# A diffusion step with two scans per head: the first levels of the scans set between the products of the paired projections

## The chip, the cores and the metric

The kernel runs on one core of a Trainium2 chip. Its engines are TensorE (PE in the profile; PEld is its loading of weights), VectorE (DVE), ScalarE (ACT), GpSimd (POOL) and SyncE (SP), which issues nearly all DMAs from one queue, in order. The metric is device time in microseconds of one execution.

## The reference, cut to what matters

One layer on 1152 tokens (128 context, 1024 latent) of width 1024. One input projection feeds eight heads of a gated scan in both directions and a Fourier branch with four groups; both are gated, projected, merged and projected once more.

```python
proj = h @ w_in
q, ff, fb, vi, zA, u, zB, gA, gB = jnp.split(proj, SPLITS, axis=-1)
qh = jax.nn.silu(heads(q)); vh = heads(vi)
logf_f, k_f = forget_gate(heads(ff), lb_f)      # k = 1 - f
logf_b, k_b = forget_gate(heads(fb), lb_b)
# per head and direction, token by token: S = diag(f) S + k v^T, o = S^T q
o = o_f + o_b_rev[:, ::-1]
o = o * lax.rsqrt(jnp.mean(o * o, axis=-1, keepdims=True) + EPS) * gnorm_w
yA = o.reshape(B, L, D_A) * jax.nn.silu(zA)
yF = jnp.fft.fft2(ug, axes=(1, 3), norm='ortho').real
yB = yF * jax.nn.silu(zB)
merged = jax.nn.sigmoid(gA) * (yA @ w_pa) + jax.nn.sigmoid(gB) * (yB @ w_pb)
return merged @ w_o, S_f, S_b
```

## The kernel before

**The stages.** A startup normalises the input and splits every value into a high and a low part, so that three products of reduced precision give one of full precision (`mm3`, lines 197 to 199: high by high, low by high, high by low). Then come the **paired projections**: 27 calls of `pair`, two output blocks of 128 columns each. A pair computes seven block products instead of eight, each for two halves j of 576 columns in slices of 288, so it has 14 products of 12 matmuls. Its weights are loaded into one buffer `raw` (512 KB twice) and turned into seven blocks: a11, a12, a22 straight from `raw`, and four sums s1 to s4 (lines 538, 540, 542, 546, VectorE). Each block is split (line 525 on ScalarE for the high part, line 526 on GpSimd for the low part). VectorE joins the seven products with seven additions for each half (line 551). An activation follows, and the result goes to DRAM. The forget gates take a Sigmoid on ScalarE and a multiply and add on GpSimd (lines 592, 593). The Fourier branch is a generator, `four`, of which the pairs run one step after each half.

**The scan stage.** Then come the eight heads. A head has six levels within blocks of 32 tokens (0, 1, 2, 4, 8, 16; `scan_blocks`): each takes 36 matmuls of 32x32 into `s_ps` (line 188), a merge into `a32` (lines 698, 700), and for the levels from 1 on two copies that pick halves (`km`, `qm`, lines 686, 688, ScalarE) and three multiplications that carry the factors on (`grow`: `qq` and `kk` at full length, line 665, and the factors `ff`, line 667, VectorE). Then `scan_rest` does the levels 32 and 64, transposes, the states S, the outputs and the normalisation.

**What sets the order.** Python generators are advanced by a string of letters for each step n (`PATTERN`): E is one level of head n, L a step of `scan_rest` of head n-1, Y a step of the end of head n-2, F one slice of the dense projections of the branches (12 matmuls of 288 columns), V half a slice of the late value projection (12 of 256 columns). The matmuls of the scan stage keep this order; a scheduler places all else by its own estimate of time, and on each engine the instructions then run in that fixed order. Before, a step n from 2 to 7 has six E, nine L, three Y and seven to nine F; there are 20 V, all in the steps 0 and 1.

## Time and profile before

| | us |
|---|---|
| median of 3 runs (1364.75 to 1376.12) | 1366.0 |
| the profiled execution | 1369.38 |
| its span in the trace | 1367.6 |
| mean granted clock of TensorE | 0.954 of 2.4 GHz |

The trace has its times from the start of the span. The startup ends at about 160 us, the paired projections at 806.6, the scan stage at about 1195, and the rest is the last branch products and the output projection.

### The profile page before, as it was taken

The page shows a single profiled execution, that of the slowest core. Times are in us where ns is not written, and L with a number is a line of the kernel's source. Part 1 is how long each engine was busy: PE and PEld are TensorE (multiplying, and loading weights), DVE is VectorE, ACT ScalarE, POOL GpSimd, SP SyncE. Part 2 cuts the span into 40 slices and gives each one's busy share as a digit, 9 for nine tenths or more (in the row PEclk, how much of TensorE's full clock was granted, in tenths as well). Part 3 has the DMA queues.
Part 4 walks back from the last instruction along what each step waited for, and adds up shares of the span by engine and source line. Part 5 has one row for each costly group of instructions (what it writes and reads, how often), then busy time and mean ns, then how long its engine had stood idle before and what let it go on. Part 6 is the DMA issues. An engine that isn't in the chain of part 4 may idle for free. (4 is left out here: it accounts for less than half of the span.)

```text
span 1367.6 us, 31165 instructions
## 1 busy us (share of the span) xinstructions
PE 1257.8 (92%) x12768; PEld 1189.8 (87%) x12768; DVE 853.0 (62%) x1403; ACT 569.4 (42%) x1056; POOL 658.7 (48%) x499
## 2 busy tenths in 40 slices
PE   5999899999999999999999996878787787999998
PEld 2679899999999999999999996877786786999886
DVE  7737744444344344444443478999999999675554
ACT  4542223333333233323332446666666664432332
POOL 4426546555647456558643503321312734464654
PEclk8899999999999999999999998898988898999999
DMA  8542242332443443233423243553445433577332
GB/s 321 195 170 73 69 140 84 119 135 91 130 133 117 154 153 114 84 114 109 157 93 113 85 157 107 179 156 113 138 147 172 119 117 100 153 219 234 119 129 99
DMA packets 102993, 185.04 MB, mean 135 GB/s; under 512 B 9777, under 2 KB 70978, under 8 KB 99650
## 3 DMA queue, kind: packets, MB, share of 16 engines
q1 hardware_dynamic: 102562, 182.00, 40.6%
q8 instruction: 100, 1.64, 0.5%
q10 hardware_dynamic: 288, 1.05, 0.3%
q14 instruction: 43, 0.35, 0.1%
HBM read 132.41 MB, written 50.60 MB: 134 GB/s over the span
## 5 line engine op out<-in xcount | busy, mean ns | idle before, releaser
L174 POOL TENSOR_TENSOR w_lo<-w_raw,w_hi 128x512 fp32r<-128x512 f32 (+1 forms) x36 | 78.7, 2188 | 194.3 <-ACT w_hi L172 164.1
L842 POOL TENSOR_TENSOR merged<-merged,gs 128x288 f32<-128x288 f32 x64 | 72.2, 1138 | 65.6 <-DVE gs L841 65.5
L188 PE MATMUL d_ps<-yh,w_hi 128*128 128x288 f32 x256 | 86.7, 339 | 10.7 <-DVE merged L839 4.9
L665 DVE TENSOR_TENSOR qq<-qq,ff 128x1152 f32<-128x1152 f32 x56 | 91.9, 1653 | 6.9 <-ACT qm L688 6.7
L542 DVE TENSOR_TENSOR sb<-raw 128x512 f32<-128x512 f32 x27 | 21.5, 798 | 112.6 <-DMA raw<-in_w_pr 112.6
L665 DVE TENSOR_TENSOR kk<-kk,ff 128x1152 f32<-128x1152 f32 x56 | 89.9, 1605 | 0.3
L188 PE MATMUL d_ps<-yh,w_lo 128*128 128x288 f32 x256 | 80.6, 315 | 0.5 <-POOL w_lo L174 0.5
L188 PE MATMUL d_ps<-yl,w_hi 128*128 128x288 f32 x256 | 80.5, 314 | 0.0
L593 POOL TENSOR_SCALAR c<-c,omlb,lb 128x576 f32<-128x576 f32 x32 | 28.1, 879 | 107.3 <-ACT c L592 60.5
L526 POOL TENSOR_TENSOR a11l<-raw,a11h 128x512 fp32r<-128x512 f32 x27 | 34.9, 1294 | 74.8 <-ACT a11h L525 74.7
L188 PEld LDWEIGHTS d_ps<-yh,w_hi 128*128 128x128 f32 x256 | 52.9, 207 | 13.5 <-ACT w_hi L172 3.9
L551 DVE TENSOR_TENSOR c<-o_ps,u 128x288 f32<-128x288 f32 x108 | 48.9, 453 | 23.4 <-PE o_ps L199 22.0
L584 ACT ACTIVATE sg<-c 128x576 f32<-128x576 f32 x40 | 27.4, 685 | 84.8 <-DVE c L551 82.4
L551 DVE TENSOR_TENSOR u<-o_ps,m 128x288 f32<-128x288 f32 x36 | 16.3, 454 | 74.3 <-PE o_ps L199 70.3
L686 ACT COPY km<-kk 128x1152 f32<-128x1152 f32 x40 | 51.9, 1297 | 14.3 <-DVE kk L665 7.5
L688 ACT COPY qm<-qq 128x1152 f32<-128x1152 f32 x40 | 52.1, 1302 | 10.1 <-PE s_ps L188 7.1
L188 PE MATMUL o_ps<-S,qq 128*128 128x128 f32 x256 | 44.2, 295 | 12.5 <-DVE S L767 12.5
L188 PEld LDWEIGHTS d_ps<-yh,w_lo 128*128 128x128 f32 x256 | 53.0, 207 | 0.9 <-POOL w_lo L174 0.9
L188 PEld LDWEIGHTS d_ps<-yl,w_hi 128*128 128x128 f32 x256 | 53.4, 209 | 0.0
L526 POOL TENSOR_TENSOR s2l<-sa,s2h 128x512 fp32r<-128x512 f32 x27 | 34.9, 1294 | 32.5 <-ACT s2h L525 32.5
L667 DVE TENSOR_TENSOR ff<-ff 128x1152 f32<-128x1152 f32 (+6 forms) x56 | 50.2, 907 | 0.1
L188 PEld LDWEIGHTS s_ps<-qm,km 128*32 128x32 f32 x2880 | 33.0, 123 | 20.0 <-ACT qm L688 14.0
(405 smaller groups left out, 5044.6 us busy)
## 6 DMA issues: line engine op xcount, KB each, us to landing
raw<-in_w_pr SPq DMA_DIRECT2D x52, 512.0 KB, 4.8
gs<-g_dr SPq DMA_DIRECT2D x96, 144.0 KB, 3.1
w_raw<-in_w_pab SPq DMA_DIRECT2D x44, 256.0 KB, 3.2
f_dr<-c SPq DMA_DIRECT2D x32, 288.0 KB, 2.3
ff<-f_dr SPq DMA_DIRECT2D x8, 1152.0 KB, 6.4
wa<-in_w_ada SPq DMA_DIRECT2D x8, 1024.0 KB
g_dr<-c SPq DMA_DIRECT2D x28, 288.0 KB, 2.9
xs<-in_xT SPq DMA_DIRECT2D x6, 768.0 KB, 9.5
```

The costliest lines, as they stand in the source:

```text
L174: eng.tensor_tensor(out=lo, in0=raw, in1=hi.bitcast(F32), op=ALU.subtract)
L188: queued(nc.tensor.matmul(*args, **kw))
L526: nc.gpsimd.tensor_tensor(out=lo, in0=src, in1=hi.bitcast(F32), op=ALU.subtract)
L542: nc.vector.tensor_tensor(out=sb, in0=a11, in1=a21, op=ALU.subtract)
L551: nc.vector.tensor_tensor(out=out, in0=m, in1=x, op=ALU.add)
L584: nc.scalar.activation(sg, c, AF.Sigmoid)
L593: nc.gpsimd.tensor_scalar(out=c, in0=c, scalar1=omlb[:, i:i + 1], scalar2=lb[:, i:i + 1], op0=ALU.mult, op1=ALU.add)
L665: nc.vector.tensor_tensor(out=xv, in0=xv, in1=view(ff2, off, [[2 * m, T // (2 * m)], [step, 2], [0, m]]), op=ALU.mult)
L667: nc.vector.tensor_tensor(out=fv[0], in0=fv[0], in1=fv[1], op=ALU.mult)
L686: nc.scalar.copy(km.rearrange("p (b i m) -> p b i m", i=2, m=m), view(kk2, 0, dims))
L688: nc.scalar.copy(qm.rearrange("p (b i m) -> p b i m", i=2, m=m), view(qq2, 0, dims))
L842: nc.gpsimd.tensor_tensor(out=out, in0=out, in1=gs, op=ALU.add)
```

## The change

The levels 0, 1, 2 and 4 of all heads leave the scan stage and become a second generator, `pieces`, that is run after `fourier` by the same calls inside the pairs. A head's tokens are cut into two pieces of 640 and 512. A piece loads its factors and q from DRAM, makes `kk`, `qq` and `k0`, does the four levels (with 20 or 16 matmuls each), and stores `kk`, `qq`, the merged blocks and every eighth factor (`fa`) to DRAM. A pair now calls the generator three times in each half (after the products 5, 7 and 2) from the eighth pair on, twice in the pairs 3 to 7. So a piece takes five calls, the 16 pieces 80, at six a pair.

The scan stage loads `kk`, `qq` and `fa` (2.6 MB a head instead of 1.7 MB) into one of three sets of buffers, one head ahead, and does only the levels 8 and 16; `grow` reads the short factors. `PATTERN` has two E in a step, and eight F in each of the steps 2 to 7; the V are ten and ten.

In the pairs, the low parts of the four sums s1 to s4 are made by VectorE, not GpSimd; the third sum is written over `raw`; the second step of the forget gates is done by ScalarE. The pairs that need the Fourier result (zB) are now the last two, behind the gates, and the buffers that hold that result are those into which head 0 is loaded.

```diff
-PATTERN = ['VVVVEEVVVEVVVEVVEVVEVV', 'LEVLEVLLEVVLLEFEFLLLEF', 'LFEFYYYFLEFLLEFLLEFEFLLLEFF', 'LEYYYFLEFLLEFLLEFEFLLLEFF', 'LEFYYYFLFELLEFLLEFEFLLLEFF', 'LEFYYYFLEFLLEFLLEFEFLLLEFF', 'LEFYYYFLFELLEFLLEFEFLLLEFF', 'ELFYYYFLEFLLEFLLEFEFLLELFF', 'LYYFYFLFLLFLLFLLLFFF', 'YFYYFFF']
+EARLY = (1, 2, 4)
+LATE = (8, 16)
+GRAN = 8
+PIECES = ((0, 640), (640, T))
+PATTERN = ['VVVVVVVVEVVE', 'LVVELVVLEVVLVVLVVLFLFLFLF'] + 6 * ['LFEYLFYLFYELFLFLFLFLFL'] + ['LFYLFYLFYLFLFLFLFLFLF', 'YFYFYFF']
 HW = T // 2
+W0 = 1280
+FA = 2 * T // GRAN
...
+    def load_head(p, hd, tags=("kk", "qq", "fa")):
+        kk, qq = (p.tile([P, 2, T], F32, tag=t, name=t) for t in tags[:2])
+        nc.sync.dma_start(kk, kk_dr[hd])
+        nc.sync.dma_start(qq, qq_dr[hd])
+        fa = p.tile([P, FA + NCH * 32], F32, tag=tags[2], name="fa")
+        nc.sync.dma_start(fa, fa_dr[hd])
+        return kk, qq, fa[:, :FA], fa[:, FA:].rearrange("p (c t) -> p c t", t=32)
...
+    def grow(ff, kk, qq, m, w=T, g=1):
+        n, mg, wg = w // (2 * m), m // g, w // g
+        dims = [[2 * m, n], [w + m, 2], [1, m]]
+        for x, off, step in ((qq, wg + mg, -(wg + mg)), (kk, mg, wg - mg)):
+            xv = view(x, 0, dims)
+            nc.vector.tensor_tensor(out=xv, in0=xv, in1=view(ff, off, [[2 * mg, n], [step, 2], [0, m]]), op=ALU.mult)
+        fv = [view(ff, o, [[wg, 2], [2 * mg, n]]) for o in (0, mg)]
+        nc.vector.tensor_tensor(out=fv[0], in0=fv[0], in1=fv[1], op=ALU.mult)
+    def halves(x, km, m, w=T):
+        nc.scalar.copy(km.rearrange("p (b i m) -> p b i m", i=2, m=m), view(x, 0, [[2 * m, w // (2 * m)], [w + m, 2], [1, m]]))
+    def merge(a32, m, ps, n):
+        pv = ps[:, :n * 32].rearrange("p (c t) -> p c t", t=32)
+        if m == 0:
+            nc.vector.tensor_tensor(out=a32, in0=pv, in1=m_d.unsqueeze(1).broadcast_to([P, n, 32]), op=ALU.mult)
+        else:
+            nc.vector.copy_predicated(out=a32, mask=m_i[:, LEVELS.index(m), :].unsqueeze(1).broadcast_to([P, n, 32]), data=pv)
+    def within(ps, km, qm, n, mm):
+        for c in range(n):
+            for j in range(4):
+                ts = slice(c * P + 32 * j, c * P + 32 * j + 32)
+                mm(ps[32 * j:32 * j + 32, c * 32:c * 32 + 32], lhsT=km[:, ts], rhs=qm[:, ts], start=True, stop=True)
...
+    def pieces():
+        x = lp.tile([P, 2, W0], F32, tag="qq", name="px")
+        z = lp.tile([P, 2, W0], F32, tag="kk", name="pz")
+        sm_ = lp.tile([P, 2, 257], F32, tag="tab", name="ps").rearrange("p a b -> p (a b)")
+        todo = [(hd, t0, t1) for hd in range(NH) for t0, t1 in PIECES]
+        def load(hd, t0, t1):
+            w = t1 - t0
+            nc.sync.dma_start(x[:, 0, :2 * w].rearrange("p (d t) -> p d t", d=2), f_dr[hd, :, :, t0:t1])
+            nc.sync.dma_start(z[:, 1, :w], q_dr[hd, :, t0:t1])
+        load(*todo[0])
+        for i, (hd, t0, t1) in enumerate(todo):
+            w, n = t1 - t0, (t1 - t0) // P
+            ff, qq, kk, q, k0 = x[:, 0, :2 * w], x[:, 1, :2 * w], z[:, 0, :2 * w], z[:, 1, :w], z[:, 1, w:2 * w]
+            a32 = sm_[:, :n * 32].rearrange("p (c t) -> p c t", t=32)
+            fa = sm_[:, n * 32:n * 32 + 2 * w // GRAN].rearrange("p (d t) -> p d t", d=2)
+            for d in range(2):
+                ds, es = slice(d * w, (d + 1) * w), slice((1 - d) * w, (2 - d) * w)
+                nc.scalar.activation(kk[:, ds], ff[:, ds], AF.Identity, bias=ones[:, 0:1], scale=-1.0)
+                nc.vector.tensor_tensor(out=qq[:, es], in0=q, in1=ff[:, ds], op=ALU.mult)
+            nc.vector.tensor_tensor(out=k0, in0=kk[:, :w], in1=kk[:, w:], op=ALU.add)
+            yield
+            for m in (0,) + EARLY:
+                if m:
+                    halves(kk, k0, m, w)
+                    halves(qq, q, m, w)
+                    grow(ff, kk, qq, m, w)
+                ps = scan_ps()
+                within(ps, k0, q, n, nc.tensor.matmul)
+                merge(a32, m, ps, n)
+                if m == EARLY[-1]:
+                    nc.scalar.copy(fa, ff.rearrange("p (d t) -> p d t", d=2)[:, :, 0:w:GRAN])
+                    nc.sync.dma_start(kk_dr[hd, :, :, t0:t1], kk.rearrange("p (d t) -> p d t", d=2))
+                    nc.sync.dma_start(qq_dr[hd, :, :, t0:t1], qq.rearrange("p (d t) -> p d t", d=2))
+                    nc.sync.dma_start(fa_dr[hd, :, :FA].rearrange("p (d t) -> p d t", d=2)[:, :, t0 // GRAN:t1 // GRAN], fa)
+                    nc.sync.dma_start(fa_dr[hd, :, FA + t0 // P * 32:FA + t1 // P * 32], sm_[:, :n * 32])
+                    if i + 1 < len(todo):
+                        load(*todo[i + 1])
+                yield
+    four = chain(fourier(), pieces())
...
-            nc.gpsimd.tensor_tensor(out=lo, in0=src, in1=hi.bitcast(F32), op=ALU.subtract)
+            eng = nc.vector if tag[0] == "s" else nc.gpsimd
+            eng.tensor_tensor(out=lo, in0=src, in1=hi.bitcast(F32), op=ALU.subtract)
...
-            sb = sp.tile([P, 4, P], F32, name="sb")
             w = {1: split(a11, "a11")}
             nc.vector.tensor_tensor(out=sa, in0=a21, in1=a22, op=ALU.add)
             w[5] = split(sa, "s1")
             nc.vector.tensor_tensor(out=sa, in0=sa, in1=a11, op=ALU.subtract)
             w[6] = split(sa, "s2")
-            nc.vector.tensor_tensor(out=sb, in0=a11, in1=a21, op=ALU.subtract)
-            w[7] = split(sb, "s3")
+            nc.vector.tensor_tensor(out=a21, in0=a11, in1=a21, op=ALU.subtract)
+            w[7] = split(a21, "s3")
...
+                    if i in (() if n < 3 else (5, 4) if n < 8 else (5, 7, 2)):
+                        next(four, None)
...
-                if n > 2:
-                    next(four, None)
...
-                nc.gpsimd.tensor_scalar(out=c, in0=c, scalar1=omlb[:, i:i + 1], scalar2=lb[:, i:i + 1], op0=ALU.mult,
-                                        op1=ALU.add)
+                nc.scalar.activation(c, c, AF.Identity, bias=lb[:, i:i + 1], scale=omlb[:, i:i + 1])
...
+        for j in range(1, KT):
+            pair(n, ((sigmoid, g_dr[0, j]), (sigmoid, g_dr[1, j])))
+            n += 1
+        for _ in four:
+            pass
+        yfs = [lp.tile([P, 2, T], F32, tag=t, name="yfs") for t in ("kk", "qq")]
...
-        first = load_head(lp, 0)
+        first = load_head(lp, 0, ("kk", "qq", "tab"))
...
-    def scan_blocks(hd, ff, q):
...
+    def scan_blocks(hd, kk, qq, fa, a32):
+        kk2, qq2 = flat(kk), flat(qq)
+        for m in LATE:
+            km = s0[0].tile([P, T], F32, name="km", bufs=2)
+            halves(kk2, km, m)
+            qm = s0[0].tile([P, T], F32, name="qm", bufs=1)
+            halves(qq2, qm, m)
+            grow(fa, kk2, qq2, m, g=GRAN)
+            within(ps, km, qm, NCH, matmul)
+            merge(a32, m, ps, NCH)
+            if m == LATE[-1]:
+                heads[hd] = (fa, kk, qq, a32)
...
+    loaded = [first, load_head(s0[0], 1)]
     for n in range(NH + 2):
-        blocks = scan_blocks(n, *(load_head(s2 if n % 2 else lp, n) if n else first)) if n < NH else iter(())
+        if 0 < n < NH - 1:
+            loaded.append(load_head((lp, *s0)[(n + 1) % 3], n + 1, ("kk", "qq", "fa" if (n + 1) % 3 else "tab")))
+        blocks = scan_blocks(n, *loaded[n]) if n < NH else iter(())
```

**In the pairs, TensorE.** The rows are matmuls of the products of two blocks (`h1h`, `h2h` are high parts of the input, `s4h`, `a12h` of a block). Before, one product follows the other:

```order
L197 MATMUL o_ps<-h1h_137,a12h 128x288
L198 MATMUL o_ps<-h1l_138,a12h 128x288
L199 MATMUL o_ps<-h1h_137,a12l 128x288
L197 MATMUL o_ps<-h1h_139,a12h 128x288
L198 MATMUL o_ps<-h1l_140,a12h 128x288
L199 MATMUL o_ps<-h1h_139,a12l 128x288
L197 MATMUL o_ps<-h2h_149,s4h 128x288
```

and in the changed kernel:

```order
L206 MATMUL d_ps<-h2h_156,s4h 128x288
L207 MATMUL d_ps<-h2l_157,s4h 128x288
L208 MATMUL d_ps<-h2h_156,s4l 128x288
L206 MATMUL d_ps<-h2h_158,s4h 128x288
L481 MATMUL s_ps<-pz 32x32 x20
L207 MATMUL d_ps<-h2l_159,s4h 128x288
L208 MATMUL d_ps<-h2h_158,s4l 128x288
L206 MATMUL o_ps<-h1h_128,a11h 128x288
```

The 20 small matmuls of one level of one piece (`pz` holds its `kk` and `q`) now stand between the matmuls of a product.

**In the pairs, VectorE and SP's queue.** One pair's stretch on VectorE (`c` and `u` are the additions of products, `m_...` the first product copied; `sa`, `sb` the sums). Before:

```order
L546 TENSOR_TENSOR sa<-raw,sa 128x512
L551 TENSOR_TENSOR c<-o_ps,m_4831 128x288
L551 TENSOR_TENSOR c<-d_ps,u_4834 128x288
L542 TENSOR_TENSOR sb<-raw 128x512
L551 TENSOR_TENSOR u_4989<-d_ps,m_4988 128x288
L538 TENSOR_TENSOR sa<-raw 128x512
L551 TENSOR_TENSOR u_4990<-o_ps,u_4989 128x288
L551 TENSOR_TENSOR c<-o_ps,u_4990 128x288
L551 TENSOR_TENSOR u_4991<-o_ps,u_4989 128x288
L551 TENSOR_TENSOR c<-o_ps,u_4990 128x288
L588 SCALAR_TENSOR_TENSOR c<-c,small,sg 128x576
L551 TENSOR_TENSOR c<-d_ps,m_4988 128x288
```

and in the changed kernel, around the end of one piece and the start of the next (`px` holds its factors and `qq`):

```order
L474 COPY_PREDICATED ps<-m_i,s_ps 128x160
L634 TENSOR_TENSOR c<-d_ps,u_4823 128x288
L610 TENSOR_TENSOR s1l<-sa,s1h 128x512
L623 TENSOR_TENSOR sa<-sa,raw 128x512
L634 TENSOR_TENSOR u_4979<-d_ps,m_4978 128x288
L580 TENSOR_TENSOR px<-pz,px 128x512 x2
L581 TENSOR_TENSOR pz<-pz 128x512
L610 TENSOR_TENSOR s2l<-sa,s2h 128x512
L634 TENSOR_TENSOR u_4980<-o_ps,u_4979 128x288
L610 TENSOR_TENSOR s3l<-raw,s3h 128x512
L629 TENSOR_TENSOR sa<-raw,sa 128x512
L634 TENSOR_TENSOR c<-o_ps,u_4980 128x288
```

SP's queue in the changed kernel, at the same kind of place:

```order
L595 DMA fa_dr<-ps 128x2x64
L596 DMA fa_dr<-ps 128x128
L568 DMA px<-f_dr 128x2x640
L569 DMA pz<-q_dr 128x640
L657 DMA q_dr<-c 256x1x288
L617 DMA raw<-in_w_pr 128x1024 x2
```

The low parts s1l, s2l, s3l and the piece's multiplications now stand among the additions; the loads of the next piece stand behind the stores of the last one, and the next pair's weights (`raw`) behind those loads.

**In the scan stage, VectorE.** From the first two rows of the states S on. Before:

```order
L764 COPY ns<-o_ps 128x128 x2
L767 SCALAR_TENSOR_TENSOR S<-S,tot,o_ps 128x128 x2
L667 TENSOR_TENSOR ff<-ff 128x288
L767 SCALAR_TENSOR_TENSOR S<-S,tot,o_ps 128x128 x2
L665 TENSOR_TENSOR kk<-kk,ff 128x72x2x8
L767 SCALAR_TENSOR_TENSOR S<-S,tot,o_ps 128x128 x2
L700 COPY_PREDICATED a_12297<-m_i,s_ps 128x288
L767 SCALAR_TENSOR_TENSOR S<-S,tot,o_ps 128x128 x5
L839 TENSOR_TENSOR merged<-gs,d_ps 128x288
L665 TENSOR_TENSOR qq<-qq,ff 128x72x2x8
L767 SCALAR_TENSOR_TENSOR S<-S,tot,o_ps 128x128 x2
L700 COPY_PREDICATED a_12297<-m_i,s_ps 128x288
```

and in the changed kernel:

```order
L815 COPY ns<-o_ps 128x128 x2
L818 SCALAR_TENSOR_TENSOR S<-S,tot,o_ps 128x128 x4
L890 TENSOR_TENSOR merged<-gs,d_ps 128x288
L818 SCALAR_TENSOR_TENSOR S<-S,tot,o_ps 128x128 x10
L890 TENSOR_TENSOR merged<-gs,d_ps 128x288
L841 RECIPROCAL ss<-ss 128x3
L890 TENSOR_TENSOR merged<-gs,d_ps 128x288
L843 TENSOR_TENSOR on<-o_ps,ss 128x384
L841 RECIPROCAL ss<-ss 128x3
L890 TENSOR_TENSOR merged<-gs,d_ps 128x288
L843 TENSOR_TENSOR on<-o_ps,ss 128x384
```

Between the states and the outputs of one head there are now no `grow` and no merge of the next head's levels.

## Rows read from the trace of the kernel before

**Rows 1.** The page: busy time by engine; slices of VectorE and granted clock.
```profile
PE 1257.8 (92%) x12768; PEld 1189.8 (87%) x12768; DVE 853.0 (62%) x1403; ACT 569.4 (42%) x1056; POOL 658.7 (48%) x499
...
DVE  7737744444344344444443478999999999675554
...
PEclk8899999999999999999999998898988898999999
```

**Rows 2.** Busy time by stretch: two pairs, five heads' steps, the last step.
```profile
core 0: us, PE busy (x) PEld busy (x) DVE busy (x) ACT busy (x) POOL busy (x), PEclk, DMA share, GB/s
480.00:527.00 47.00, 47.00 (x357) 47.00 (x356) 21.83 (x40) 15.86 (x27) 25.80 (x21) 1.00 0.42 141
905.00:1145.00 240.00, 193.41 (x3824) 182.07 (x3824) 228.79 (x330) 149.46 (x280) 77.49 (x42) 0.87 0.45 137
1163.50:1193.00 29.50, 27.15 (x314) 26.28 (x313) 18.94 (x41) 14.44 (x43) 15.68 (x12) 1.00 0.57 172
```

**Rows 3.** VectorE in order of time: the totals that end each head's level 64.
```profile
910.30 0.16 DVE L740 COPY tot<-ff 128x18 f32<-128x18 f32 x1
...
1142.39 0.17 DVE L740 COPY tot<-ff 128x18 f32<-128x18 f32 x1
...
1179.85 0.71 DVE L740 COPY tot<-ff 128x18 f32<-128x18 f32 x1
```

**Rows 4.** TensorE in order of time: the first late value matmuls, one level's group.
```profile
806.58 0.27 PE L188 MATMUL d_ps<-vh,h1h 128*128 128x256 f32 x1
...
809.44 0.28 PE L188 MATMUL d_ps<-vh,h1h 128*128 128x256 f32 x1
...
884.90 0.83 PE L188 MATMUL s_ps<-qm,km 128*32 128x32 f32 x72
885.66 0.40 PE L188 MATMUL d_ps<-yh,w_hi 128*128 128x288 f32 x1
885.89 0.29 PE L188 MATMUL d_ps<-yl,w_hi 128*128 128x288 f32 x1
886.02 0.29 PE L188 MATMUL d_ps<-yh,w_lo 128*128 128x288 f32 x1
```

**Rows 5.** Groups by line and shape, 905 to 1145 us; one line's minimum, median, maximum.
```profile
L665 DVE TENSOR_TENSOR qq<-qq,ff 128x1152 f32<-128x1152 f32 x38 | 60.9, 1615 | 4.1 <-ACT qm L688 4.0
L700 DVE COPY_PREDICATED a<-m_i,s_ps 128x288 f32<-128x288 int32 x27 | 13.0, 481 | 0.0
L667 DVE TENSOR_TENSOR ff<-ff 128x1152 f32<-128x1152 f32 x5 | 8.4, 1688 | 0.0
L667 DVE TENSOR_TENSOR ff<-ff 128x288 f32<-128x288 f32 x5 | 3.6, 717 | 0.0
L686 ACT COPY km<-kk 128x1152 f32<-128x1152 f32 x27 | 34.7, 1286 | 5.5 <-DVE kk L665 5.4
...
L665 DVE TENSOR_TENSOR qq<-qq,ff x40: 1339/1357/3040, 904.5 to 1157.3; 128x1152 f32<-128x1152 f32 x40
```

**Rows 6.** Durations (ns, minimum/median/maximum) of two sums of the pairs; groups there.
```profile
L546 DVE TENSOR_TENSOR sa<-raw,sa x23: 679/1433/1905, 262.6 to 781.7; 128x512 f32<-128x512 f32 x23
L540 DVE TENSOR_TENSOR sa<-sa,raw x23: 679/691/1757, 259.4 to 778.6; 128x512 f32<-128x512 f32 x23
...
L526 POOL TENSOR_TENSOR s4l<-sa,s4h 128x512 fp32r<-128x512 f32 x23 | 29.7, 1291 | 0.2 <-ACT s4h L525 0.2
L586 POOL TENSOR_TENSOR c<-c,sg 128x576 f32<-128x576 f32 x22 | 31.9, 1452 | 23.0 <-ACT sg L584 23.0
L592 ACT ACTIVATE c<-c 128x576 f32<-128x576 f32 x30 | 20.6, 686 | 58.4 <-DVE c L551 44.0 <-issue 14.3
```

**Rows 7.** VectorE in order of time: a full-length multiplication and the instruction behind it.
```profile
1144.74 1.34 DVE L665 TENSOR_TENSOR qq<-qq,ff 128x1152 f32<-128x1152 f32 x1
1146.01 0.44 DVE L841 TENSOR_TENSOR gs<-gs,d_ps 128x288 f32<-128x288 f32 x1
```

**Rows 8.** DMA issues on the page: the load of a head's factors, KB, us to landing.
```profile
ff<-f_dr SPq DMA_DIRECT2D x8, 1152.0 KB, 6.4
```

More of the change, by code (lines that the diff above doesn't have):

```diff
@@ L1 @@
 from contextlib import ExitStack, contextmanager
-from itertools import cycle
+from itertools import chain, cycle
 import numpy as np
@@ L516, in fourier @@
                 yield
-    four = fourier()
+    def pieces():
[36 more added lines that the diff above has]
+                yield
@@ L627, in diffusion_step @@
             n += 1
-        for j in range(1, KT):
-            pair(n, ((sigmoid, g_dr[0, j]), (sigmoid, g_dr[1, j])))
-            n += 1
-        first = load_head(lp, 0)
+        first = load_head(lp, 0, ("kk", "qq", "tab"))
         tstack.close()
@@ L724, in scan_rest @@
             nc.scalar.copy(att[r, :, o:o + 32], ps[r, :NCH * 32].rearrange("p (c t) -> p c t", t=32))
-        grow(ff, kk, qq, 32)
+        grow(fa, kk2, qq2, 32, g=GRAN)
         yield
@@ L1070, in _layout @@
         names += [("q", h), ("ff", h), ("fb", h), ("zA", h)]
-    names += [("zB", g) for g in range(NG)]
     for j in range(1, KT):
         names += [("gA", j), ("gB", j)]
+    names += [("zB", g) for g in range(NG)]
     w_pr = blocks(np.concatenate([blk[k][:, i] for k, i in names], 1), 2 * P)
```

73 lines of the change are left out of this document (15 added, 58 removed).

## The prediction

> **What bounds the kernel now.** I read the page first: TensorE is busy 92% of the span, VectorE 62% [rows 1]. The slices show that this mean hides two different stages. VectorE stands at four tenths for the whole of the paired projections and at nine tenths in the scans, and there alone the granted clock of TensorE falls below full [rows 1]. The busy time by stretch makes it exact [rows 2]. In two pairs (47 us, so 23.5 a pair) TensorE is busy all the time at the full 2.4 GHz, VectorE 21.83, ScalarE 15.86, GpSimd 25.80 us. In 240 us of the scans VectorE is busy 228.79 (95%), TensorE 193.41 at a mean granted clock of 0.87. So the pairs are bound by TensorE, the scans by VectorE, and the change carries work of both from the second to the first. What it is worth is the scans' loss of VectorE time less what TensorE and VectorE lose in the pairs.
>
> The last step of the scans shows the scan stage without any level: 29.5 us, TensorE 27.15 busy at a clock of 1.00, VectorE only 18.94 [rows 2].
>
> **The scan stage, part by part.** I cut it by the totals that end each head's level 64 [rows 3]; the products of the pairs end where the first late value product begins, at 806.6 [rows 4].
>
> 1. *From head 1 to head 6:* 910.30 to 1142.39, five steps of 46.4 us [rows 3]. Each step loses four levels. By the rows this is, on VectorE, three pairs of full-length multiplications, two products q f and one addition for k0 (nine, recorded with a median of 1.35 [rows 5], while the next instruction starts 1.27 after one [rows 7]), three products of factors (1.69 the largest, 0.72 the smallest, 3.6 in all), four merges of 0.48 less the same overlap: 11.4 + 3.6 + 1.6 = 16.6 us of a step in which it is busy 44. What is late next is TensorE and the chain of the head itself. The step that is left is the last step, 29.5 us with about as many dense slices, and two levels. A level's 36 small matmuls (72 records) take 0.76 us until the next matmul starts, and the first matmul behind them 0.23 instead of 0.13 [rows 4]; I take 0.95 with the entry. If only TensorE counts, the step is 29.5 + 1.9 = 31.4. If all VectorE time of the two levels (each two multiplications, a short product of factors of about 0.3 and a merge: 3.5) adds to the chain of the head, it is 29.5 + 7.0 = 36.5. VectorE then has 26 us of work and TensorE 29, so I take a value nearer the lower end, 33.5: 12.9 us saved five times, **65** (50 to 75).
> 2. *From the end of the pairs to head 1's total:* now 910.30 - 806.6 = 103.7 us. After the change it holds 20 V (two are 24 matmuls, 2.86 us [rows 4]: 28.6), one head's steps with some five slices instead of eight (29.5 less 3 x 12 x 0.13 = 24.8) and five levels (4.8): 58 us. Head 0 must now be loaded into buffers that the last pair still reads, two transfers of 1152 KB at 6.4 us [rows 8], while eight V cover 11.4 us: I add 10 for this and the levels that follow at once. 68, **36** saved (24 to 46).
> 3. *Head 6 to head 7:* 37.5 us now, of which part had levels: 33.5, **4** saved (0 to 6).
>
> Behind it nothing changes: the same slices are left, and TensorE is the fuller engine there. Sum of the scan stage: 105 saved (74 to 127). The larger loads of a head (2.6 instead of 1.7 MB) are issued a head ahead, and so cost nothing; if they came late, ScalarE's copies would wait as they would for any load, some 6 us a head.
>
> **The pairs, part by part.**
>
> 4. *TensorE:* 64 groups of 20 or 16 small matmuls. Half of 0.76 us is 0.38, and with the same entry and exit as above (0.2) a group costs 0.58, for here nothing hides it, TensorE having no idle time: **37** lost (24 with no cost of switching, 49 if a half group costs as much as a whole one).
> 5. *VectorE:* a pair has 10.9 us of it now [rows 2]. Four low parts come to it, at the 0.69 of a difference of that shape [rows 6] less the overlap: 2.5. A piece and a fifth a pair, or 0.6 of a head, brings 0.6 x 17.7 (the 16.6 above, and 1.1, an estimate of mine for doing each of 16 operations twice in halves, from that 0.07 of each that isn't work): 10.6. Sum 24.0 us against 26.3 for TensorE (23.5 + 4.8 x 0.58). TensorE stays the bound by a small margin, but VectorE goes in order, and behind each of the piece's multiplications stand additions that free PSUM for the next product. So some of it will show: two busy engines at 92% and 100% don't mesh without gaps. Bounds: 0 if they do, and 60 (4.5 us in each of the 13.3 pairs that hold the 80 calls) if VectorE's time is stretched as below. I take **15**, nearer to zero, since the sum of VectorE's row is below TensorE's.
> 6. *GpSimd and ScalarE:* GpSimd loses four low parts of 1.29 us [rows 6] and the gates' second step, from 12.9 to about 7 us a pair. ScalarE goes from 7.9 to about 15.5 (two activations of 0.69 [rows 6] for the gates; eight copies of about 1.29 [rows 5] for a head, 0.6 of a head a pair). Both are hidden under TensorE's 26; with no cover the gates' step would cost 0.7 us.
> 7. *DMA:* 4.3 MB a head more in the pairs, 34 MB in 313 us, or 110 GB/s beside 141 at a busy share of 0.42 [rows 2]. It fits, with a share near 0.75. Each piece's load stands in SP's queue behind the last piece's stores and ahead of the next pair's weights; the price of that is in the third rival.
>
> A row shows what VectorE's margin is exposed to: the same difference of 512 elements takes 0.69 us (median) at line 540 and 1.43 at line 546, where GpSimd makes a low part beside it [rows 6]. The nearest rows thus give 0.74 us a meeting. With GpSimd's time halved and VectorE's tripled I count some two or three meetings a pair, 2 us, which leaves 26.0 against 26.3. The Trainium skill (SBUF — State Buffer, "SBUF: two separate sides") states that the two engines share one pair of ports under an exclusive lock, and that the loser is blocked for the whole instruction of the other; the two medians agree with a block, though of part of GpSimd's 1.29 us only. By that rule at its worst each of GpSimd's operations left in a pair would be a full block; this is the second rival.
>
> **The sum.** The profiled execution took 1369.4 us (span 1367.6): 1369.4 - 105 + 37 + 15 = 1316.4. The median of the runs is 3.4 below the profiled one, so I forecast **1313**.
>
> **The rivals.**
>
> - *No gaps at all:* steps of 31.4, the start at 58, half groups at 0.38 and VectorE hidden. 1369.4 - 75 - 46 - 6 + 24 = 1266, or 1272 if the switches cost half of what I took; median 1263 to 1269. For it: at the end TensorE is busy 27.15 of 29.5 even in a chain of one head. Against: in every stretch where two engines are full some time is lost. Chance 0.12.
> - *VectorE becomes the bound of the pairs:* each of three low parts and of one product by GpSimd in a pair blocks VectorE for its whole length: 3 x 1.29 + 1.45 = 5.3 us [rows 6], so 24.0 + 5.3 = 29.3. An engine that bounds is busy 95% [rows 2]: 30.8 us a pair, 13.3 x 7.3 = 97 lost instead of 52: 1361 profiled, median 1358. For it: line 546. Against: half of the runs of line 540 show no such meeting [rows 6]. Chance 0.13.
> - *Slower, by the loads of the pieces:* factors and q have one buffer, so a piece's load starts only when the last one has its last product of factors, and VectorE's first multiplication of the next piece waits for it with low parts and additions queued behind. TensorE runs out of PSUM and of weights. At 6.4 us each, the landing time of a load nearly twice as large [rows 8], 16 pieces cost 102: 1369.4 - 105 + 37 + 102 = 1403, median 1400. It decides from (105 - 37) / 16 = 4.3 us a piece. For it: the queue order and the higher DMA share. Against: four to six instructions (some 4 us) and a product stand between the two, and TensorE has several products of slack. Chance 0.07.
> - *The scans don't shrink as far:* the head's chain, not VectorE, holds the step at 41: 5 x 5.4 + 25 saved, 52 lost, 1369; with 38 it is 1352, median 1349. Against it is the last step, which is that chain. Chance 0.08. That the change doesn't do what it says can be left out, since the order shows the groups between the products.
>
> **How the numbers follow.** The forecast has 0.60: its own range, from the bounds of the terms, is about 1283 to 1345. The range that leaves out no more than two in ten cuts the first rival and the third (0.19) and takes in the second: 1270 to 1360. A measurement of this kernel can't tell less than 1% from no change, so faster means below 1352 and slower above 1380. Faster: 0.60 + 0.12 + 0.08, as half of the fourth rival and a rest of the second fall here: 0.80. Same 0.12, slower 0.08.
>
> **What would show it.** In the profile after: steps of the scans near 33.5 us between totals, with VectorE below 85% and the granted clock near 1; pairs of about 27.4 us where the pieces run, VectorE near 90%, TensorE with little idle time; the s_ps groups there of some 0.4 to 0.6 us; TensorE's busy time about unchanged. Wrong would be: pairs of 30 us or more with TensorE waiting for sums (second rival), VectorE waiting for px (third), steps of 38 or more (fourth).

## The result, and the profile after

The changed kernel takes 1363.3 us (median of 12 runs, 1356.95 to 1369.57) against 1369.5 of the kernel before beside it: a ratio of 0.9947 [0.9927, 0.9968]. That is half a per cent faster, where 1313 was forecast, and 3 us above the range. Its profiled execution took 1363.05 us (span 1361.3) at a mean granted clock of 0.971 (0.954 before).

The page of the changed kernel, the lines that answer to [rows 1]:

```profile
PE 1260.5 (93%) x12768; PEld 1183.7 (87%) x12768; DVE 922.2 (68%) x1639; ACT 601.3 (44%) x1168; POOL 470.0 (35%) x359
...
DVE  7737755545468878889878787547767676565554
...
PEclk7899899999999999899999999989999899999999
```

VectorE's plateau of nines in the scans is gone; in its place stands one of eights in the second half of the pairs. The work went where it was sent, and the granted clock rose in the scans.

Busy time by stretch after (columns as in [rows 2]): pairs without pieces; most of the sixteen pairs with them (they run from 397 to 834.7); from the end of the pairs to head 0's total; to head 1's; to head 6's.

```profile
166.60:233.98 67.38, 67.38 (x515) 67.33 (x515) 34.42 (x68) 17.95 (x34) 18.48 (x16) 1.00 0.36 118
...
404.00:835.00 431.00, 405.01 (x4945) 388.75 (x4947) 356.75 (x610) 221.97 (x364) 87.41 (x56) 0.98 0.49 161
887.00:935.00 48.00, 33.97 (x585) 32.14 (x584) 29.66 (x34) 22.64 (x34) 17.70 (x10) 0.86 0.58 213
935.00:976.00 41.00, 36.65 (x491) 34.91 (x492) 25.98 (x48) 20.24 (x50) 14.16 (x9) 0.96 0.69 219
976.00:1144.00 168.00, 149.04 (x2235) 143.25 (x2223) 118.38 (x239) 92.39 (x232) 58.22 (x42) 0.97 0.64 209
```

In the scans' middle VectorE fell from 95% to 70% and TensorE rose from 81% to 89%, at a clock of 0.97. In the pairs with pieces TensorE is no longer always busy: 26 of 431 us are gaps.

The first late value product and the totals after, in order of time, as [rows 3, 4]:

```profile
886.93 0.28 PE L197 MATMUL d_ps<-vh,h1h 128*128 128x256 f32 x1
...
934.77 0.15 DVE L791 COPY tot<-fa 128x18 f32<-128x18 f32 x1
975.93 0.18 DVE L791 COPY tot<-fa 128x18 f32<-128x18 f32 x1
1144.32 0.18 DVE L791 COPY tot<-fa 128x18 f32<-128x18 f32 x1
1172.76 0.71 DVE L791 COPY tot<-fa 128x18 f32<-128x18 f32 x1
```

They give the account, in us of the two profiled executions:

| stretch | before | after | saved | predicted |
|---|---|---|---|---|
| up to the end of the pairs | 806.6 | 886.9 | -80.4 | -52 (terms 4, 5) |
| end of the pairs to head 1's total | 103.7 | 89.0 | 14.7 | 36 (term 2) |
| head 1 to head 6, five steps | 232.1 | 168.4 | 63.7 | 65 (term 1) |
| head 6 to head 7 | 37.5 | 28.4 | 9.0 | 4 (term 3) |
| head 7 to the end of the span | 187.8 | 188.5 | -0.8 | 0 |

So 28 of the 47 us that are missing were lost in the pairs and 21 at the start of the scans; the rest, terms 1 and 3 and the tail, makes up for 3.

In the timeline of the changed kernel one group of a piece stands among a pair's products:

```profile
726.09 0.30 PE L208 MATMUL o_ps<-t2h,s3l 128*128 128x288 f32 x1
726.23 0.29 PE L206 MATMUL o_ps<-t2h,s3h 128*128 128x288 f32 x1
726.45 0.46 PE L481 MATMUL s_ps<-pz 128*32 128x32 f32 x32
726.84 0.40 PE L207 MATMUL o_ps<-t2l,s3h 128*128 128x288 f32 x1
727.08 0.29 PE L208 MATMUL o_ps<-t2h,s3l 128*128 128x288 f32 x1
```

Products of this shape start every 0.13 us (0.133 in the mean of that product); from the one ahead of the group to the second behind it are 0.85, so the group of 16 took 0.85 - 2 x 0.133 = 0.58. One of 20, at 797.53, took 0.69; over the groups with no gap ahead of them these are the medians too. That is 64 x 0.64 = 41 us.

What VectorE waited for in the pairs with pieces (397 to 835 us; us in total, times, longest):

```profile
DVE sa L621 <- DMA raw<-in_w_pr: 25.3, 12, 4.3
DVE px L580 <- DMA pz<-q_dr: 17.8, 11, 3.6
DVE pz L461 <- ACT pz L467: 14.8, 18, 1.3
DVE s1l L610 <- ACT s1h L608: 9.0, 4, 3.0
```

Weights, a piece's load, ScalarE's halves and ScalarE's high parts: 67 us in which VectorE stood, with the rest of its order queued behind. In the kernel before, the weights were waited for as well (40 us from 560 to 750 us), but VectorE then had little else due: it was busy 21.83 of 47 us [rows 2].

What TensorE waited for in the same stretch, all of it:

```profile
PE s_ps L481 <- issue: 8.7, 9, 1.9
PE d_ps L206 <- DVE u L634: 6.1, 5, 2.1
PE s_ps L481 <- ACT pz L467: 4.7, 8, 0.9
PE o_ps L206 <- DVE u L634: 3.4, 2, 1.8
PE s_ps L481 <- DVE pz L581: 2.9, 1, 2.9
```

Of these 26 us, 16 stand ahead of a piece's own group (`s_ps`) and 9.5 ahead of a product whose PSUM an addition (`u`) had still to free. The nine without a releaser ("issue") are the first groups of pieces: each began 0.10 us after VectorE's addition for `k0` (line 581) had ended. So TensorE, which takes its matmuls in order, mostly stood for the piece's operands and less for the additions.

The gaps had a second price. The granted clock fell to the lower level (1.2 GHz) four times in this stretch, for 17 us in all, each time during or behind one of the longer gaps (1.8 to 2.9 us). The first time, with the gap ahead of it, and the longest:

```profile
463.00:465.50 2.50, 0.68 (x6) 0.47 (x5) 2.50 (x5) 0.01 (x1) 0.81 (x1) 1.00 0.00 0
466.40:469.70 3.30, 3.30 (x52) 2.96 (x51) 3.20 (x6) 3.30 (x5) 0.00 (x0) 0.50 0.65 211
551.70:558.40 6.70, 6.10 (x55) 6.07 (x56) 5.84 (x11) 3.04 (x4) 0.00 (x0) 0.50 0.71 245
```

At half the clock 17 us lose 8.5. The groups (41), the gaps (26) and the clock (8.5) make 75 of the 80 us that the pairs lost.

### The profile page after: what moved, and what is told of

The parts are those of the page before. It is cut to its first block, busy times and chain, and to the rows that moved or that the text cites. A ratio compares the mean times of both kernels' runs of the same rounds, so it can differ in the third digit from the quotient of the medians.

```text
span 1361.3 us, 31510 instructions
## 1 busy us (share of the span) xinstructions
PE 1260.5 (93%) x12768; PEld 1183.7 (87%) x12768; DVE 922.2 (68%) x1639; ACT 601.3 (44%) x1168; POOL 470.0 (35%) x359
## 4 chain that ended last, share of the span: by engine, by line
PE 28%; DMA 9%; DVE 7%; issue 3%; ACT 3%; POOL 2%; SPq 1%; DVEq 0%; ACTq 0%; POOLq 0%
PE d_ps L197 6%; PE o_ps L197 5%; DMA raw<-in_w_pr 3%; PE o_ps L208 3%; PE o_ps L207 3%; PE o_ps L206 3%; DMA wr<-in_w_o 3%; PE o_ps L200 1%; PE d_ps L206 1%; PE d_ps L208 1%; DVE kk L461 1%; PE d_ps L207 1%; DMA qq<-qq_dr 1%; DVE qq L461 1%; POOL a12l L610 1%
## 5 line engine op out<-in xcount | busy, mean ns | idle before, releaser
L669 POOL TENSOR_TENSOR c<-c,sg 128x576 f32<-128x576 f32 x24 | 36.3, 1514 | 140.4 <-ACT sg L667 81.1
L610 POOL TENSOR_TENSOR a22l<-raw,a22h 128x512 fp32r<-128x512 f32 x27 | 39.0, 1443 | 112.5 <-ACT a22h L608 112.5
L461 DVE TENSOR_TENSOR qq<-qq,fa 128x1152 f32<-128x1152 f32 x32 | 45.3, 1427 | 23.3 <-ACT qm L467 13.0
L667 ACT ACTIVATE sg<-c 128x576 f32<-128x576 f32 x40 | 27.4, 685 | 73.6 <-DVE c L634 70.1
L610 POOL TENSOR_TENSOR a12l<-raw,a12h 128x512 fp32r<-128x512 f32 x27 | 41.8, 1549 | 51.8 <-ACT a12h L608 44.6
L461 DVE TENSOR_TENSOR pz<-pz,px 128x640 f32<-128x640 f32 (+1 forms) x48 | 47.5, 990 | 15.1 <-ACT pz L467 14.8
L634 DVE TENSOR_TENSOR c<-o_ps,u 128x288 f32<-128x288 f32 x108 | 48.5, 449 | 10.8 <-PE o_ps L208 10.3
L181 ACT CAST w_hi<-w_raw 128x512 fp32r<-128x512 f32 (+1 forms) x48 | 34.8, 725 | 47.2 <-DMA w_raw<-in_w_pab 15.3
L467 ACT COPY pz<-pz 128x640 f32<-128x640 f32 (+1 forms) x48 | 37.7, 785 | 33.8 <-PE s_ps L481 22.3
L461 DVE TENSOR_TENSOR kk<-kk,fa 128x1152 f32<-128x1152 f32 x32 | 50.9, 1608 | 0.7
L481 PEld LDWEIGHTS s_ps<-pz 128*32 128x32 f32 x2304 | 26.2, 113 | 27.9 <-issue 20.1
L481 PE MATMUL s_ps<-pz 128*32 128x32 f32 x2304 | 33.1, 200 | 16.4 <-issue 8.7
```

Of the source, the lines that this page charges most:

```text
L461: nc.vector.tensor_tensor(out=xv, in0=xv, in1=view(ff, off, [[2 * mg, n], [step, 2], [0, m]]), op=ALU.mult)
L467: nc.scalar.copy(km.rearrange("p (b i m) -> p b i m", i=2, m=m), view(x, 0, [[2 * m, w // (2 * m)], [w + m, 2], [1, m]]))
L481: mm(ps[32 * j:32 * j + 32, c * 32:c * 32 + 32], lhsT=km[:, ts], rhs=qm[:, ts], start=True, stop=True)
L610: eng.tensor_tensor(out=lo, in0=src, in1=hi.bitcast(F32), op=ALU.subtract)
L634: nc.vector.tensor_tensor(out=out, in0=m, in1=x, op=ALU.add)
L669: nc.gpsimd.tensor_tensor(out=c, in0=c, in1=sg, op=ALU.mult)
```

## The experiments: the pairs

A yardstick for single profiles: from the start of the 8th pair's first weight cast to the 26th's are 421.05 us in the kernel before and 490.84 in the changed one:

```profile
343.87 0.62 ACT L608 CAST a11h<-raw 128x512 fp32r<-128x512 f32 x1 [0.73 <-PE o_ps L207]
...
834.71 0.61 ACT L608 CAST a11h<-raw 128x512 fp32r<-128x512 f32 x1
```

Two kernels below that change nothing in the pairs (with more value products ahead, and without head 0's loads) show 485.0 and 488.6. Less than some 6 us there says nothing. The theories: A, a piece is a chain through one set of buffers, as long as the pair; B, VectorE's work sets the pair; C, the groups' own time on TensorE is the loss; D, which comes later, a piece costs a pair some 5 us whatever its work. Each edit in the pairs also lets the scheduler place the pieces anew, so each run shows the edit together with its new order.

**The low parts back on GpSimd.**

```diff
-            eng = nc.vector if tag[0] == "s" else nc.gpsimd
+            eng = nc.gpsimd
```

> The changed kernel, with the low parts of the four sums back on GpSimd; all else as changed. The changed kernel stands at 0.995 of the kernel before, and its 16 pairs that hold a piece last 27.4 us each against 22.25 for a plain pair. Theory A (a piece is one chain through one set of buffers, which is as long as the pair): the low parts are not in that chain, the pairs stay at 27 to 28 us, ratio 0.99 to 1.00. Theory B (VectorE's work sets the pair): 2.5 to 3.5 us of work leave VectorE in each pair, the pairs fall to about 25.5 us and the ratio to about 0.973.

Measured: 1378.8 us, 1.0081 [1.0057, 1.0105]. The stretch is 502.6 us, 12 longer. Of it, by VectorE's waits:

```profile
DVE px L580 <- DMA pz<-q_dr: 28.0, 8, 6.5
...
DVE sa L623 <- POOL s1l L610: 12.2, 9, 2.7
...
DVE sa L629 <- POOL s2l L610: 4.7, 10, 0.7
```

VectorE has less to do (340.83 us in 397 to 845) and waits more: sa is one buffer, and the next sum can only be written once GpSimd has read the last for its low part. So VectorE's work by itself isn't the price; what it waits for in its order is part of it. TensorE's gaps ahead of the pieces' groups grew from 16 to 34 us, those for additions fell from 9.5 to 2.4.

**Only the first piece is loaded.** The 15 other loads are left out; the same values are worked on again.

```diff
-                    if i + 1 < len(todo):
-                        load(*todo[i + 1])
```

> The changed kernel, in which only the first piece loads its factors and q; the 15 others compute with what lies in the buffers, so that the scans get wrong numbers and the time is that of the same work without 15 loads. Theory A: each piece's chain loses the 5 us between the last product of factors and the landing of the load, the pairs fall to the 24.8 us that TensorE needs (22.25 and four groups of 0.64), 16 x 2.5 = 40 us, ratio 0.966. Theory B: no VectorE work goes, the pairs stay near 27, ratio 0.99.

Measured: 1373.0 us, 1.0037 [1.0021, 1.0053]; the stretch is 496.4. The pieces stand closer (they end in the 23rd pair, pairs then take 22.4) at 28.6 us a pair, and the sum is no smaller. So the loads make a piece last as long as a pair, but aren't what it costs: theory A falls as far as it rests on them. The chain through one set of buffers isn't gone, though. The next piece now waits for the stores of the last one, ScalarE 20.4 us for that of `kk` and VectorE 10.3 for that of `qq` (399 to 771 us), which it didn't in the changed kernel. While the pieces run, VectorE is busier than in the changed kernel, 85%:

```profile
399.00:771.00 372.00, 341.92 (x4376) 327.08 (x4376) 318.01 (x536) 201.58 (x324) 80.21 (x49) 0.98 0.39 134
```

**One wide matmul in place of a group.** It leaves out most products of the pieces, by shape and count.

```diff
-                within(ps, k0, q, n, nc.tensor.matmul)
+                nc.tensor.matmul(ps[:, :n * 32], lhsT=k0[:, :P], rhs=q[:, :n * 32], start=True, stop=True)
```

> The changed kernel, in which each of the 64 groups of 20 or 16 small matmuls in the pairs is one wide matmul of 160 or 128 columns into the same bank; the levels 0, 1, 2 and 4 come out wrong, everything else is done. Theory C (the groups' own time on TensorE is the loss): 64 x (0.64 - 0.15) = 31 us back, ratio 0.972. Theory A: the chain loses only the difference of a group's length, four times 0.3 us a piece, 16 x 1.2 = 19 us, ratio 0.981. Theory B: nothing, 0.99 to 0.995.

Measured: 1364.9 us, 0.9971 [0.9956, 0.9985]; the stretch is 472.65, 12 to 18 shorter, and the total isn't. The gain was lost behind the stretch: the pieces now end in the last pair, which takes 42.7 us up to the first late value product instead of 30.4. There (835 to 885 us) TensorE stood once for an addition, and VectorE for a store, which in the changed kernel cost VectorE 2.9 us and TensorE nothing:

```profile
PE o_ps L206 <- DVE c L634: 10.2, 1, 10.2
...
DVE c L634 <- DMA yb_dr<-c: 9.3, 1, 9.3
```

Nor was all of the groups' time taken away. The one wide matmul with its entry and exit takes 0.27 us in the median, so the edit frees some 64 x (0.64 - 0.27) = 24 of 41 us, and half of that to three fourths came back. The rest went into waiting: in its pairs VectorE is busy 346.89 of 420 us, 83% as in the changed kernel, and TensorE's gaps grew from 26 to 31.5 us. So theory C holds for a part of the loss, and the total of this run can't be used against it.

**The pieces without their multiplications by decays.**

```diff
                     halves(qq, q, m, w)
-                    grow(ff, kk, qq, m, w)
```

> The pieces leave out their 9 multiplications by decays each (the levels' growing), so their output is not the reference's; products, copies, loads and stores stay. Theory B (VectorE's queue, work and blocked waits together, sets the pairs with pieces at 27.4 us): VectorE loses about 7 us a pair, TensorE's 22.4 + 2.6 = 25 us becomes the bound, the pairs from the 8th to the 26th fall from 490.8 to 450-460 us, total 1325-1335. Theory D (a piece costs about 5 us of each pair whatever its work, as a chain of loads, copies and products handed between engines): 480-491 us, total 1353-1363.

Measured: 1339.0 us, 0.9779 [0.9756, 0.9802]; the stretch is 462.0, 23 to 29 shorter, the largest step of the four. Its stretch from 402 to 806 us:

```profile
402.00:806.00 404.00, 394.72 (x4958) 380.98 (x4957) 245.52 (x472) 222.89 (x365) 80.25 (x56) 1.00 0.55 179
```

VectorE is at 61%, TensorE has 9 us of gaps and a clock of 1.00. The last five pairs take 22.2 to 22.4: the pieces are through in 13 to 14 pairs, as they are written, not 16. Theory B by itself expected 450 to 460 and a total of 1325 to 1335; it came 2 and 4 us short of that. Theory D expected 480 or more. So VectorE's work in the pieces, in its order, is worth 23 to 29 of the 70 us, and the gaps and the lower clock go with it. What stays over the kernel before, 41 us, is of the size that the timeline gives for the groups on TensorE. The two together are 64 to 70 of the 70 us.

## The experiments: the scans

**A fourth level in the pairs.**

```diff
-EARLY = (1, 2, 4)
-LATE = (8, 16)
-GRAN = 8
+EARLY = (1, 2, 4, 8)
+LATE = (16,)
+GRAN = 16
```

> A fourth level is taken from the scans into the pieces. The scans lose one level of two: 3.2 us a head as the first four gave, 24 us, if a step still shrinks. In the pairs: theory C (TensorE's groups are the price) adds 16 x 0.64 = 10 us, total 1349; theory B (VectorE's queue) adds 16 x 2.4 us (three multiplications and a merge) = 39 us, total 1378; the price per level that the change has shown so far (82 us for 4 levels of 8 heads) adds 20 us, total 1360; theory D adds next to nothing, total 1340.

Measured: 1422.3 us, 1.0387 [1.0365, 1.0409], outside all of them, and for a reason that none had: with one more call a piece the pieces weren't through when the pairs with products were, and the rest ran without any:

```profile
835.00:940.00 105.00, 63.21 (x879) 59.95 (x878) 63.88 (x107) 37.93 (x62) 29.09 (x19) 0.76 0.42 145
1032.00:1178.00 146.00, 124.14 (x1556) 119.68 (x1555) 81.47 (x176) 69.30 (x182) 37.87 (x30) 0.94 0.62 207
```

The pairs ended at 940.7, 54 later. As a test of a level's price it is spoilt. It does show something of the scans: with half the levels left, the five steps from head 1 to head 6 took 36.6, 37.1, 34.5, 38.1 and 27.4 us, 34.7 in the mean, not less than the 31.9, 31.9, 35.0, 37.5 and 32.0 of the changed kernel (33.7), though VectorE is at 56%. (TensorE's clock was 0.94 there against 0.97, by estimate about 1 us of a step.) As the steps are written, taking more work off VectorE gave nothing there. Whether the written order of the steps, which was left as it was, holds them was not tried.

**Six more value products ahead of head 0's first step.**

```diff
-PATTERN = ['VVVVVVVVEVVE', 'LVVELVVLEVVLVVLVVLFLFLFLF'] + 6 * ['LFEYLFYLFYELFLFLFLFLFL'] + 
...
+PATTERN = ['VVVVVVVVVVVVVVEVVE', 'LVELVLEVLVLLFLFLFLF'] + 6 * ['LFEYLFYLFYELFLFLFLFLFL'] + 
...
```

> Six more of the late V projections stand before head 0's first scan step. If the start of the scans loses time because head 0's loads are issued and land late (TensorE idle 14 of the first 45 us), these cover the landing: end of pairs to head 0's total stays 48 or grows while head 0's to head 1's falls by more, together 5-10 us less, total 1353-1358. If the start is bound by VectorE's and ScalarE's chain of the two heads, their work starts later by what the six take, and the total is the same or 5 longer.

Measured: 1365.7 us, 0.9969 [0.9949, 0.9989]: no gain. End of the pairs to head 0's total 51.3, to head 1's 40.9, to head 2's 34.5 (47.8, 41.2, 31.9 in the changed kernel).

**Without head 0's two large loads.** Its scan reads what the buffers hold.

```diff
-        first = load_head(lp, 0, ("kk", "qq", "tab"))
+        fa_t = lp.tile([P, FA + NCH * 32], F32, tag="tab", name="fa")
+        nc.sync.dma_start(fa_t, fa_dr[0])
+        first = (yfs[0], yfs[1], fa_t[:, :FA], fa_t[:, FA:].rearrange("p (c t) -> p c t", t=32))
```

> Leaves out the two large loads of head 0 (its scan reads what stands in the buffers, so that its output is not the reference's). Theory F (the start of the scans loses its time to head 0's transfers, which are asked for late and land after 11 us: ScalarE waits 15.7 us for them, TensorE 12 us behind it): end of pairs to head 1's total falls from 89 to 77-81 us, total 1351-1355. Theory G (TensorE's own work of some 70 us and the chain of the two heads' steps hold the stretch): 85-89 us, total 1359-1363.

The loads looked guilty. In the changed kernel, 880 to 935 us:

```profile
ACT qm L467 <- DMA qq<-qq_dr: 15.7, 1, 15.7
...
DVE qq L461 <- ACT qm L467: 11.1, 1, 11.1
DVE vo L922 <- DMA yb_dr<-c: 7.1, 1, 7.1
...
PE o_ps L200 <- DVE kk L461: 4.7, 1, 4.7
...
PE d_ps L197 <- DVE vo L922: 4.2, 2, 3.6
...
PE s_ps L197 <- ACT qm L467: 3.8, 1, 3.8
```

Measured: 1356.0 us, 0.9906 [0.9892, 0.9921]. The stretch to head 1's total is 85.2 instead of 89.0, so the loads cost 4 us there, not 8 to 12: theory G by the stretch. The total lies between the two forecasts; the other 2 to 4 us of the gain are in stretches that the edit doesn't touch. Of TensorE's three waits the one for qm is gone, but those for kk (4.7) and for the buffer vo (5.3) stay, and TensorE is busy 67.6 us of these 85.2. A long wait on ScalarE, with 11 us of VectorE behind it, was worth 4 us of the stretch.

## The experiments: the parts alone

**The kernel before, with the low parts of the four sums on VectorE and the gates' second step on ScalarE**, without moved levels (the two edits of the diff, on the kernel before).

> The kernel before, with two parts of the change alone: the low parts of the four sums on VectorE and the gates' second step on ScalarE. TensorE is busy all the time in the pairs there and VectorE only four tenths: no change, ratio 0.998 to 1.002. If the low parts on VectorE delay the additions that free PSUM, it is slower, 1.005 or more.

Measured: 1383.7 us, 1.0110 [1.0082, 1.0138]. The pairs were 2.6 us shorter, and the steps of the scans, in which nothing was edited, went from 45 to 49 us to 46 to 51.5.

**The gates alone**, and **the low parts alone**, each on the kernel before:

> The kernel before with the gates' second step on ScalarE and nothing else. VectorE's order in the scans is then that of before, line for line. If the 14 us by which the parts-only kernel was slower are the scheduler's other order of the scans, this one has scan steps of 45-49 us as before and a total of 1364-1370. If a changed load of GpSimd or ScalarE slowed the scans, steps of 47-51 us and a total above 1375.

> The kernel before with the low parts of the four sums on VectorE and nothing else. The scheduler puts some 35 instructions of VectorE in the scans in another place, as in the parts-only kernel, though none of them is changed. If that order is what cost 14 us, this one has its steps (50-52 us for four of the seven) and a total of 1378-1386, with pairs 2-4 us shorter. If not, 1364-1370.

Measured: the gates alone 1369.8 us, 1.0008 [0.9990, 1.0026], steps as before (44.7 to 48.4); the low parts alone 1385.6, 1.0106 [1.0080, 1.0132], four steps of 49.0 to 50.4. In the second kernel the programs of TensorE, ScalarE, GpSimd and SP from the first late value product on are those of the kernel before. Only VectorE's differs, by the order that the scheduler gave to instructions that nobody changed: moving 17 of its 653 turns one order into the other (- before, + low parts alone; the lines between are the same in both):

```
- L767 SCALAR_TENSOR_TENSOR S<-S,tot,o_ps 128x128
+ L668 TENSOR_TENSOR ff<-ff 128x144
...
+ L666 TENSOR_TENSOR kk<-kk,ff 128x36x2x16
...
- L665 TENSOR_TENSOR kk<-kk,ff 128x36x2x16
+ L768 SCALAR_TENSOR_TENSOR S<-S,tot,o_ps 128x128
```

An update of the state S, which TensorE's next product of S reads, now stands behind a long multiplication of another head. The waits from 910 to 1155 us show it:

```profile
ACT sq L788 <- PE o_ps L188: 34.3, 14, 8.5
...
DVE ss L791 <- ACT ss L790: 16.7, 7, 3.5
...
PE o_ps L188 <- DVE S L768: 15.6, 5, 5.5
```

In the kernel before these are 23.6, 6.6 and 7.4 us from 910 to 1142. So an edit in the pairs, which left their length as it was (640.7 us from the first weight cast to the end, 641.0 before), cost 12 us up to head 7's total and 2 behind it. The change takes that edit in; what its scans would be with another deal of their order can't be read from these runs.

## The experiments: a better version

**The gates' second step back on GpSimd** in the changed kernel (the two lines of the diff undone).

> The gates' second step goes back to GpSimd (32 x 0.88 us there, the same less on ScalarE); the low parts of the sums stay on VectorE. If what GpSimd does in the pairs is paid through VectorE and the shared chain, as giving back the low parts was (+15 us), this is 3-8 us slower; if ScalarE's queue (VectorE waits for its halves 15 us in 16 pairs) is the tighter one, 3-8 us faster.

Measured: 1357.8 us, 0.9929 [0.9906, 0.9952]; the interval overlaps the changed kernel's. At least it isn't slower.

**One low part of four back on GpSimd**, s4's or s3's:

```diff
-            eng = nc.vector if tag[0] == "s" else nc.gpsimd
+            eng = nc.vector if tag in ("s1", "s2", "s3") else nc.gpsimd
```

> Of the four low parts, that of s4 alone (0.93 us a pair on VectorE) goes back to GpSimd. Theory B (VectorE's work sets the pairs with pieces): 16 pairs x 0.93 = 15 us less there, less what the GpSimd step costs VectorE while both run (about 0.6 us a meeting), so 5-15 us faster than the changed kernel, total 1348-1358. Theory E (GpSimd's slower step in the weights' chain and its meetings with VectorE cost more than they relieve, as with all four given back, +15 us): 2-6 us slower, total 1365-1370.

> The same with s3's low part alone (1.15 us a pair on VectorE, the one used third of the seven products). Theory B: up to 18 us less in the pairs, total 1345-1358. Theory E: slower than with s4, since TensorE needs s3 earlier, total 1366-1374.

Measured: s4 1354.4 us, 0.9874 [0.9846, 0.9903], the best that was found, below the changed kernel's interval (both against the kernel before, not side by side). s3 1365.2, 0.9964 [0.9941, 0.9986]. The same kind of work was moved; what differs is the place. In the pairs of s3's kernel:

```profile
L629 DVE TENSOR_TENSOR sa<-raw,sa 128x512 f32<-128x512 f32 x16 | 20.6, 1288 | 0.3
...
L610 DVE TENSOR_TENSOR s1l<-sa,s1h 128x512 fp32r<-128x512 f32 x16 | 11.8, 737 | 13.7 <-ACT s1h L608 13.7
```

and of s4's:

```profile
L629 DVE TENSOR_TENSOR sa<-raw,sa 128x512 f32<-128x512 f32 x17 | 16.0, 940 | 0.1
...
L610 DVE TENSOR_TENSOR s1l<-sa,s1h 128x512 fp32r<-128x512 f32 x17 | 13.6, 799 | 9.0 <-ACT s1h L608 9.0
```

With s3's low part on GpSimd the sum at line 629 takes 1.29 us in the mean instead of 0.94. s4 is the last sum of a pair and its product the last of seven, so nothing of VectorE's stands behind its low part for its buffer until the next pair. That this makes the difference is argued from the order; 16 x 0.35 us is about half of the 11 us between the two kernels. **Both s4 and the gates on GpSimd:**

> Both pieces of work that were harmless or better on GpSimd are put there: s4's low part and the gates' second step. If their gains add (s4: about 13 us below the kernel before's 1368 more than the changed kernel's 6, gates: 0-5), total 1348-1353. If GpSimd's meetings with VectorE eat the second, 1354-1360, no better than with s4 alone.

Measured: 1358.3 us, 0.9901 [0.9875, 0.9928]. No gain of the second step shows: the intervals of this kernel and of s4 alone overlap, and s4 alone remains the version to take.

## Why the prediction was wrong, by its own steps

**Right: what bounds each stage of the kernel before, and term 1.** The five steps took 33.7 us in the mean, 33.5 were predicted, and by the predicted exchange: VectorE 70% and TensorE 89% at a clock of 0.97. Term 3 was 5 us too small, since the step came to 28.4, below the 29.5 taken as its floor. Term 4 was of the right size: 41 us instead of 37. Term 6 called ScalarE hidden, and mostly it is, but TensorE stood 4.7 us for its halves. Term 7 put the DMA share near 0.75; it was 0.49.

**Wrong: term 5, VectorE in the pairs.** It took 15 us where the pairs lost 39 beside the groups: 26 in gaps, 8.5 by the clock, and some 5 that no row here explains. It compared work with work, 24.0 us a pair against 26.3, and found room. The work was not underestimated: with one piece a pair its sum is 22.3, and VectorE was busy 356.75 of 431 us, so 22.6 of each pair's 27.3. But its time in a pair is its work and its waits, since it goes in order, and the four producers (weights, a piece's load, halves, high parts) took most of the other 4.7 us. In the kernel before such waits were free, as half of VectorE's time was; the step gave them no price. The run without multiplications shows it: with that work gone, waits of VectorE get longer (weights alone 46 us from 397 to 806), TensorE's gaps shrink to 9 us, and 23 to 29 us come back. The step also named the smaller way in which VectorE's lateness reaches TensorE: additions that free PSUM are 9.5 us of the gaps, while 16 are TensorE standing at the piece's own groups, which are set in its order before their operands are made. That, and the lower clock behind the gaps, no term has.

Two counts made it worse. A pair of 27.4 us with pieces was predicted, and 27.4 it is (397.0 to 834.7 holds 16 pairs, and in each a piece begins). That is luck, as two errors cancel. The base of 23.5 was read from a window that wasn't cut at the pairs' edges; the late pairs of the kernel before, which hold nothing else, start 22.2 to 22.3 us apart. So a pair lost 5.1, not 3.9. And the pieces took 16 pairs, not the 13.3 that the calls hold, since the scheduler set them further apart than they are written. 16 x 5.1 = 82 against 13.3 x 3.9 = 52 is the loss of the stage.

**Wrong: term 2, the start of the scans.** 68 us were forecast for a stretch in which TensorE is busy 70.6 us after the change (33.97 + 36.65) and idle 18.4. So of the 21 us that are missing 13 are work of TensorE, which was summed as 58, and 8 are idle time, for which 10 were set. The sum took products at full clock, where the granted clock is 0.86 at first, and a count by analogy with the last step; TensorE's work in the stretch before the change, 81.8 us of the 104 by the windows 806 to 861 and 861 to 910, would have shown it. The loads of head 0, for which the 10 us were meant, cost 4; what the other idle time waits for is shown above only in part (`kk`, `vo`).

**The rivals.** The second, VectorE becomes the bound of the pairs, came nearest: 97 us lost and 1358 against 80 and 1363. Its number is luck, though. It rested on GpSimd's blocks, 5.3 us a pair. The Trainium skill (SBUF — State Buffer, "SBUF: two separate sides") states that the loser of the shared ports is blocked for the other's whole instruction; the trace agrees that there are meetings. Of the 16 low parts of s3 in the pairs with pieces, the 8 that began while GpSimd was making a low part took 1.40 to 1.78 us, the 8 that began with GpSimd idle 0.67 to 0.68. The price is smaller than the rival's: the four low parts of a pair together take 1.0 us more than 4 x 0.68 in the mean. And giving GpSimd one more instruction a pair made the kernel faster, and VectorE's busy time stayed below the 24.0 of the sum without any block. The third rival, the loads of the pieces at 102 us, did not come, and the run without them is no faster. The first and the fourth did not come either; the fourth's second sum is 2 us off, as steps of 38 give 1354 by its own terms.

**Left open:** how much of the change's own scans is the luck of the scheduler's deal; the rest of TensorE's gaps at the start (for kk and vo); how much of each run in the pairs is the new order that came with its edit; and whether a fourth level pays if the pieces get enough calls.
